# Local attention by halves: row factors in the exponential, rotary rows gathered by transfers, masked copies of two blocks, query weight splits held back

## The chip, the cores and the metric

The kernel runs on one core of a Trainium2 chip. The metric is the device time of one execution in microseconds (us). The engines are named as in the profile: PE is TensorE (PEld its weight load), DVE is VectorE, ACT is ScalarE, POOL is GpSimd, SP is SyncE, which here only issues transfers. Each engine runs its own instructions in the order in which the program issues them; between engines, semaphores order what depends on one another.

## The reference

The reference is the trunk of a small language model with two layers, for 512 tokens with 16 meta tokens ahead of them, 1024 wide. Layer 0 mixes with gated linear attention, layer 1 with local attention over keys and values that are computed once. A gated feed-forward network stands ahead of and behind each mixer, and each part has a norm on its input and one on its output. What the change touches is layer 1's mixer (`hn` is the normalized input; 16 query heads of 64 share 4 key heads; the window is 128 tokens):

```python
q = (hn @ w_q).reshape(B, L, N_KV_HEADS, GROUP, HEAD_DIM)
q = (apply_partial_rope(q, cos, sin) * (HEAD_DIM ** -0.5)).transpose(0, 2, 3, 1, 4)
...
k_band, v_band = band(k), band(v)   # meta keys, previous block, own block
s = jnp.einsum('bkgnqd,bknsd->bkgnqs', q_blk, k_band)
mask = jnp.concatenate([
    jnp.ones((nB, WINDOW, N_META), dtype=bool),
    (j > i)[None] & (blk > 0),
    jnp.broadcast_to((j <= i)[None], (nB, WINDOW, WINDOW)),
], axis=-1)
p = sink_softmax(s, mask, sink)     # exp(s - m) / (sum + exp(sink - m))
o_real = jnp.einsum('bkgnqs,bknsd->bkgnqd', p, v_band)
...
return o @ w_out
```

Of each head's 64 rows the first 16 are turned (`apply_partial_rope`): eight rows with the cosine and sine of the eight others. For query i of a block, the key j of the previous block counts where j > i and that of its own block where j <= i; each column of the two blocks has therefore exactly one of the two visible.

## The kernel before, in words

**Order.** A small planner, `Flow`, holds a clock that each multiplication advances and a heap of jobs, which are generators that yield planned times or other jobs. The main program issues PE's work; whenever the clock passes a job's time, the job issues its next instructions. So constants such as `NORM`, `SOFT` and `LAG` settle where an instruction stands in its engine's queue, and nothing moves once the program is built.

**Weights.** Every float32 weight tile (128 x 512) is loaded by SP into one of 8 raw tiles, and split into a rounded part (ACT, L227) and a remainder (DVE, L228). A product is three multiplications of parts (`mm3s`, L163). Tiles wait in a pool of 32 pairs; `set_ahead(n, slots)` says how far ahead tiles are loaded and how many may be split, and `cap` up to which one.

**Layer 1's mixer, `swa`.** The input `x` is an `Operand`: `build` splits the residual H times the gain into two parts (ACT L429, DVE L430), for two token groups of 256, and `factors` gets each token's row factor 1/rms from sums of squares (`rstd`, small operations on POOL) and broadcasts it by a multiplication (`r_l1m`) to a tile R. `x_first` multiplies the first four units of query weights (128 rows of q each, two heads) group by group, 192 multiplications 256 wide, and `x_units` the last four 512 wide, 96 multiplications. When a unit is done and the row factors are known, `evac` calls `rope`: a shuffle (L1034) and a product (L1035) on DVE, a product and a sum on POOL (L1036, L1037), with tables multiplied by R and 1/8 (L1115).

Then come eight visits, one for each unit u of two heads. `soft(u)` multiplies queries with keys block by block (272 keys, or 144 in the first block), copies the meta keys and the own block (ACT, L1150), and lays the previous block's scores over the own block's where j > i (DVE, a predicated copy, L1151). One row of 144 thus holds all visible keys. Then the maximum (L1156), exponentials with their sums (ACT, L1161), the sink's exponential (L1162), the reciprocal (L1167), and the division, of the meta keys (`mt`, L1169, DVE) and of the rest (L1170, one head on DVE, one on POOL). `core(u)` transposes the probabilities on PE (L175), takes the own and the previous block apart with masks (DVE, L1190 and L1191), copies the meta part (ACT, L1181), multiplies with the values (22 multiplications) and splits the result (ACT L411, DVE L412). Projection work of PE stands between the steps of the visits. `out_proj` multiplies with the output weights, first units 0 to 3 (96 multiplications 512 wide), then 4 to 7 (192 that are 256 wide).

## Time and profile before

| | before |
|---|---|
| median of 3 runs (lowest, highest) | 1932.98 us (1929.79, 1935.67) |
| profiled execution, its own time | 1932.53 us |
| its span | 1930.5 us |
| granted PE clock, mean | 0.992 |
| first multiplication of the query projection | 1390.94 us |
| first 512-wide one of it | 1420.46 us |
| last multiplication of the output projection | about 1561.5 us |

The profile is taken from one execution. Its span goes from the first instruction to the last, and positions in the trace are counted from the span's start. Durations of one instruction contain its start-up, so instructions that follow each other at once overlap a little: a DVE operation of 0.69 us comes every 0.61.

### The profile page before, as it was taken

The numbers are of one execution on the slowest core, as the hardware profiler recorded it, in microseconds if no ns is written. First come the engines' busy times: TensorE is split into PE (matmuls) and PEld (weight loads), VectorE is DVE, ScalarE is ACT, GpSimd is POOL, SyncE is SP. The second block draws the span as 40 slices with busy tenths as digits, with TensorE's granted clock in tenths as the row PEclk, the third lists the DMA queues.
The fourth block names the chain that finished last, engine by engine and source line by source line (L and its number), as shares of the span: only waits on it lengthen the run. The fifth ranks groups of instructions, "written<-read, shape, count | busy, mean of one in ns | idle before, by whom it ended". The sixth has DMA issues, their size and how long they took to land.

```text
span 1930.5 us, 37342 instructions
## 1 busy us (share of the span) xinstructions
PE 1889.1 (98%) x14502; PEld 1801.1 (93%) x14502; DVE 1419.5 (74%) x2868; ACT 1002.5 (52%) x2268; POOL 223.0 (12%) x417
## 2 busy tenths in 40 slices
PE   8999999999999999999999999999998999999997
PEld 8999999999999999999999798989975798989897
DVE  7885858765465798586887786868779678868584
ACT  5553535653245565353574553535646565536363
POOL 2000000321121300000034000000352040000002
PEclk9999999999999999999999999999999999999998
DMA  4223233322113122333351223233321212333331
GB/s 165 91 91 107 91 106 98 123 67 77 56 45 110 56 72 90 106 91 105 99 175 45 66 83 115 91 112 102 123 66 34 69 36 85 95 107 104 105 115 44
DMA packets 102016, 174.61 MB, mean 90 GB/s; under 512 B 11344, under 2 KB 24144, under 8 KB 101840
## 3 DMA queue, kind: packets, MB, share of 16 engines
q1 hardware_dynamic: 101008, 171.59, 28.4%
q8 instruction: 113, 1.85, 0.4%
q10 hardware_dynamic: 832, 0.65, 0.1%
q14 instruction: 63, 0.52, 0.1%
HBM read 170.10 MB, written 2.10 MB: 89 GB/s over the span
## 4 chain that ended last, share of the span: by engine, by line
PE 82%; DVE 12%; ACT 3%; issue 2%; POOL 1%; DMA 0%; SPq 0%; DVEq 0%; ACTq 0%
PE y L163 30%; PE a L163 18%; PE x L163 14%; PE c L163 8%; PE d L163 4%; DVE raw L252 1%; DVE w L228 1%; ACT w_s L246 1%; DVE w_s L247 1%; DVE w L247 1%; PE e L163 1%; PE o L163 1%; PE po L163 1%; DVE xsl0f L723 0%; PE ps L163 0%
## 5 line engine op out<-in xcount | busy, mean ns | idle before, releaser
L247 DVE TENSOR_TENSOR w_s<-raw,w_s 128x512 fp32r<-128x512 f32 x288 | 194.1, 691 | 132.9 <-ACT w_s L246 131.0
L163 PE MATMUL y<-hidl0f,w 128*128 128x272 f32 (+1 forms) x2112 | 264.8, 287 | 3.3 <-ACT hidl0f L411 3.1
L163 PEld LDWEIGHTS y<-hidl0f,w 128*128 128x128 f32 x2112 | 261.7, 190 | 4.4 <-ACT hidl0f L411 3.5
L228 DVE TENSOR_TENSOR w<-raw,w 128x512 fp32r<-128x512 f32 x378 | 243.2, 674 | 17.2 <-ACT w L227 15.4
L163 PE MATMUL y<-hidl1f,w 128*128 128x512 f32 (+1 forms) x1344 | 251.1, 346 | 1.7 <-ACT hidl1f L411 1.4
L246 ACT ACTIVATE w_s<-raw 128x512 fp32r<-128x512 f32 x288 | 175.3, 628 | 145.2 <-DVE raw L252 141.5
L163 PEld LDWEIGHTS y<-hidl1f,w 128*128 128x128 f32 x1344 | 212.3, 188 | 36.6 <-ACT hidl1f L411 2.3
L227 ACT ACTIVATE w<-raw 128x512 fp32r<-128x512 f32 x378 | 208.1, 586 | 35.4 <-PE y L163 27.0
L407 POOL TENSOR_TENSOR acc_post<-acc_post,sq_post 128x256 f32<-128x256 f32 (+1 forms) x72 | 59.1, 821 | 1376.7 <-ACT sq_post L406 1376.1
L252 DVE TENSOR_TENSOR raw<-raw,raw 128x512 f32<-128x512 f32 x288 | 198.3, 688 | 5.5
L247 DVE TENSOR_TENSOR w<-raw,w 128x512 fp32r<-128x512 f32 x216 | 148.6, 688 | 39.5 <-ACT w L246 38.8
L246 ACT ACTIVATE w<-raw 128x512 fp32r<-128x512 f32 x216 | 134.0, 621 | 48.0 <-PE y L163 47.7
L163 PE MATMUL x<-x_l0m,w 128*128 128x272 f32 (+1 forms) x1200 | 158.1, 288 | 0.0
L163 PEld LDWEIGHTS x<-x_l0m,w 128*128 128x128 f32 x1200 | 149.3, 189 | 1.1
L589 DVE TENSOR_TENSOR Y<-y,Y 128x256 f32<-128x256 f32 (+2 forms) x176 | 82.5, 474 | 72.0 <-PE y L163 71.5
L163 PE MATMUL a<-zl0f_t,w_s 128*128 128x264 f32 x864 | 117.3, 285 | 0.0
L163 PE MATMUL a<-zl1f_t,w_s 128*128 128x256 f32 x864 | 114.5, 281 | 0.3 <-ACT c L784 0.2
L163 PEld LDWEIGHTS a<-zl0f_t,w_s 128*128 128x128 f32 x864 | 110.1, 188 | 0.2
L163 PEld LDWEIGHTS a<-zl1f_t,w_s 128*128 128x128 f32 x864 | 107.3, 188 | 1.9 <-ACT c L784 1.5
L163 PE MATMUL x<-x_l0f,w 128*128 128x256 f32 (+1 forms) x768 | 100.4, 291 | 7.2 <-ACT w L227 5.8
L163 PEld LDWEIGHTS x<-x_l0f,w 128*128 128x128 f32 x768 | 97.0, 192 | 8.5 <-ACT w L227 5.8
L163 PE MATMUL x<-x_l1f,w 128*128 128x256 f32 (+1 forms) x576 | 92.7, 320 | 0.0
(483 smaller groups left out, 3308.7 us busy)
## 6 DMA issues: line engine op xcount, KB each, us to landing
raw<-in_w_in SPq DMA_DIRECT2D x352, 256.0 KB, 2.9
raw<-in_w_out SPq DMA_DIRECT2D x96, 256.0 KB, 3.4
raw<-in_gla_in SPq DMA_DIRECT2D x50, 256.0 KB, 2.9
raw<-in_w_last SPq DMA_DIRECT2D x48, 256.0 KB, 3.1
raw<-in_w_out SPq DMA_DIRECT2D x64, 128.0 KB, 2.9
raw<-in_gla_out SPq DMA_DIRECT2D x16, 256.0 KB, 2.7
raw<-in_w_q SPq DMA_DIRECT2D x16, 256.0 KB, 3.9
raw<-in_swa_out SPq DMA_DIRECT2D x16, 256.0 KB, 2.8
```

Of the source, the lines that this page charges most:

```text
L163: inst = pe.matmul(o, lhs, rhs, start=start, stop=stop, skip_group_check=onto)
L227: act.activation(w[:, 0, :m], raw[:, :m], AF.Copy)
L228: dve.tensor_tensor(w[:, 1, :m], raw[:, :m], w[:, 0, :m].bitcast(F32), op=ALU.subtract)
L246: act.activation(w[:, 0, :512], src, AF.Copy)
L247: dve.tensor_tensor(w[:, 1, :512], src, w[:, 0, :512].bitcast(F32), op=ALU.subtract)
L252: dve.tensor_tensor(dst, dst, src, op=ALU.add)
L407: pool.tensor_tensor(sums[0][:, :n], sums[0][:, :n], t[:, :n], op=ALU.add)
L589: dve.tensor_tensor(y, p[:, :n], y, op=ALU.add)
```

## The change

Query rows leave PSUM by an ACT copy with the factor 1/8 (`evac`), without the row factors. `factors` makes only a column of the row factors and of their inverses (`root`), and the row factor is the scale of the exponential; the sink, times the inverse, is a 145th score. The rotary rows, 16 of every 64, are gathered by eight transfers into one packed tile, turned there by four DVE operations, and sent back by eight transfers (`turn`; two groups of 256 for the first four units, one of 512 for the last). The eight visits become sixteen, each a unit by half of the blocks, four units' first halves ahead of their second halves. Scores of two blocks lie in one PSUM tile, so one ACT copy and one predicated copy serve two blocks. The transposed probabilities are copied whole by ACT, and multiplied with the previous block's values; the masked own part goes with the difference of the two blocks' values (`dv`). POOL's part of the division goes to DVE, and so do POOL's two operations of the key's `rope`. The visits are spaced by `PERIOD` and may run `LAG` ahead. The query weights of units 4 to 7 are capped (`cap`) and split within 12 tiles (`held`), and the second half of the output projection waits only for the visits of its tokens (`second`).

The core of the diff; of `swa`, whose old body is shown above, only the new lines:

```diff
-STAGGER = 5.0
-SOFT = 5.0
+SOFT = 6.0
 BEHIND = 2.2
-NORM = 3.0
-LAG = 3
+NORM = 4.0
+LAG = 5
+PERIOD = 5.0
+TURN = 6.0
+PROBS = 2.5
...
-    def rstd(sq, n, dim, half, name, eng=pool, more=0.0):
+    def root(sq, n, dim, name, eng, yv=None, inverse=None):
...
+        if inverse is not None:
+            eng.tensor_tensor(inverse, aa, yy, op=ALU.mult)
+        return yy
+
+    def rstd(sq, n, dim, half, name, eng=pool, more=0.0):
+        yy = root(sq, n, dim, name, eng)
...
         def factors(self, gi, eng=pool):
+            if self.column is not None:
+                o, n = self.groups[gi]
+                yield FACT
+                root(self.accs[gi], n, D, f"{self.name}_{o}", eng, *self.column[gi])
+                yield CHAIN
+                return
...
             for g, p in zip(groups, pst):
-                if all(job.done for job in x.rjob):
+                if raw or all(job.done for job in x.rjob):
                     evac(i, g, p)
...
-    def x_first(x, nu, evac, opening=False, behind=(), first_ahead=8):
+    def x_first(x, nu, evac, opening=False, behind=(), first_ahead=8, held=None):
...
-        set_ahead(8 if opening else 2 * first_ahead)
+        set_ahead(8 if opening else 2 * first_ahead, held)
...
-            yield x.rjob[gi]
+            if x.column is None:
+                yield x.rjob[gi]
...
             if gi == 0 and some[-1] == nu - 1:
-                cap[0] = len(units)
+                if held is None:
+                    cap[0] = len(units)
                 prefetch()
...
         for gi, g in enumerate(split_groups):
+            if gi:
+                flow.wait(*second)
             for m in range(KD - tailm, KD):
...
         dve.stream_shuffle(sh, p, ROT_SHUFFLE)
         dve.tensor_tensor(dst, p, c, op=ALU.mult)
-        pool.tensor_tensor(sh, sh, s, op=ALU.mult)
-        pool.tensor_tensor(dst, dst, sh, op=ALU.add)
+        dve.tensor_tensor(sh, sh, s, op=ALU.mult)
+        dve.tensor_tensor(dst, dst, sh, op=ALU.add)
...
+            dve.tensor_tensor(dv, vt[:, 1:], vt[:, :3], op=ALU.subtract)
...
     def swa(x, kv, finish):
+        kz, vt, dv, vmz = kv
+        cap[0] = used[0] + 8
         with tc.tile_pool(name="ap", bufs=1) as ap:
             mgt = ap.tile([P, P], I32, name="mgt")
             sp.dma_start(mgt, a["mgt"])
+            mle = ap.tile([P, P], F32, name="mle")
             sp.dma_start(mle, a["mle"])
+
             neg = ap.tile([P, P], F32, name="neg")
+            pool.memset(neg, 0.0)
+            for r in (0, 64):
+                pool.memset(neg[r : r + 1], NEG)
             cr, sr = duo("csq")
+            sp.dma_start(cr, a["cosp"])
+            sp.dma_start(sr, a["sinp"])
+            qd = [None] * 4
 
             def evac(u, g, p):
                 o, n = g
+                if qd[u // 2] is None:
+                    qd[u // 2] = pair_tile(f"q{u}", F32)
+                act.activation(qd[u // 2][:, u % 2, o : o + n], p[:, :n], AF.Copy, scale=0.125)
+
+
+            def turn(half, g, after_jobs):
+                for jb in after_jobs:
                     yield jb
+                o, n = g
+                pk, sh = (t[:, o : o + n] for t in duo(f"turn{half}_{o}"))
+                ends = []
+                for d in range(2):
+                    for e in range(2):
+                        for c in range(2):
+                            at = 64 * d + 32 * e + 16 * c
+                            rows = qd[2 * half + d][64 * e : 64 * e + 16, c, o : o + n]
+                            ends.append((rows, pk[at : at + 16]))
+                for rows, packed in ends:
+                    sp.dma_start(packed, rows)
+                yield TURN
+                while (1, KD - 1) not in x.ready:
+                    yield SCORE
+                first = dve.stream_shuffle(sh, pk, TURN_SHUFFLE)
+                after(x.built, first)
+                dve.tensor_tensor(pk, pk, cr[:, o : o + n], op=ALU.mult)
+                dve.tensor_tensor(sh, sh, sr[:, o : o + n], op=ALU.mult)
+                dve.tensor_tensor(pk, pk, sh, op=ALU.add)
+                for rows, packed in ends:
+                    sp.dma_start(rows, packed)
+                yield TURN
+
+
+            visits = [(u, hf) for us in (range(4), range(4, KD)) for hf in range(2) for u in us]
+
+            def score_tile(i):
+                u, hf = visits[i]
+                t = flat(Y)[:, i * 580 : (i + 1) * 580] if i < 7 else flat(pair_tile(f"s{u}_{hf}", F32))[:, :580]
+                return t.rearrange("p (c t) -> p c t", t=145)
+
+            def soft(i, after_jobs):
+                for jb in after_jobs:
+                    yield jb
+                u, hf = visits[i]
                 j = u // 4
+                qq = qd[u // 2][:, u % 2]
+                s = score_tile(i)
+                nm, den = (sm.tile([P, 4], F32, tag=t, name=f"{t}{u}_{hf}", bufs=4) for t in ("nm", "den"))
+
+                rows = [slice(64 * e, 64 * e + 64) for e in range(2)]
+                pa, pb = ([ps(f"s{n}{u}_{hf}{e}") for e in range(2)] for n in "ab")
+                for c in range(2):
+                    b = 2 * hf + c
+                    qs = [qq[rows[e], META + b * P : META + (b + 1) * P] for e in range(2)]
                     for e in range(2):
+                        mm(pa[e][:, c * 144 : (c + 1) * 144], qs[e], kz[j][rows[e], b], cost=0.1)
+                    for e in range(2):
+                        o = pb[e][:, c * P : (c + 1) * P]
+                        if b:
+                            mm(o, qs[e], kz[j][rows[e], b - 1, META:], cost=0.085)
+                        else:
+                            mm(o, ones[rows[e]], neg[rows[e]], cost=0.085)
+                for e in range(2):
+                    t = s[:, 2 * e : 2 * e + 2]
+                    act.activation(t[:, :, :144], pa[e][:, :288].rearrange("p (c k) -> p c k", k=144), AF.Copy)
+                    dve.copy_predicated(
+                        t[:, :, META:144], mgt.unsqueeze(1).to_broadcast([P, 2, P]),
+                        pb[e][:, : 2 * P].rearrange("p (c k) -> p c k", k=P),
+                    )
+                while x.rjob[hf] is None:
                     yield SCORE
+                yield x.rjob[hf]
+
+                rc, ri = x.column[hf]
+                pairs = lambda t: t.rearrange("p (e c) -> p e c", c=2)
+                both = lambda t: t.unsqueeze(1).to_broadcast([P, 2, 2])
+                sinks = vec[:, V_SINK + 2 * u : V_SINK + 2 * u + 2].unsqueeze(2).to_broadcast([P, 2, 2])
+                dve.tensor_tensor(pairs(s[:, :, 144]), sinks, both(ri), op=ALU.mult)
+                dve.tensor_reduce(nm, s, axis=AX.X, op=ALU.max, negate=True)
+                dve.tensor_tensor(pairs(nm), pairs(nm), both(rc), op=ALU.mult)
+                for c in range(4):
+                    act.activation(
+                        s[:, c], s[:, c], AF.Exp, scale=rc[:, c % 2 : c % 2 + 1], bias=nm[:, c : c + 1],
+                        accum_out=den[:, c : c + 1],
+                    )
                 yield SOFT
+                dve.reciprocal(den, den)
+                rd = den.unsqueeze(2)
+                mt = sm.tile([P, 4, META], F32, tag="mt", name=f"mt{u}_{hf}", bufs=4)
+                dve.tensor_tensor(s[:, :, META:144], s[:, :, META:144], rd.to_broadcast([P, 4, P]), op=ALU.mult)
+                dve.tensor_tensor(mt, s[:, :, :META], rd.to_broadcast([P, 4, META]), op=ALU.mult)
+                probs[i] = s, mt
+
+            def core(i):
+                yield softs[i]
                 yield NORM
+                u, hf = visits[i]
                 j = u // 4
+                s, mt = probs[i]
+                pm = ps(f"ptm{u}_{hf}")
+                transpose(pm[:64, :P], mt.rearrange("p c m -> p (c m)"))
+                ptm = sm.tile([64, P], F32, tag="ptm", name=f"pm{u}_{hf}", bufs=2)
+                act.activation(ptm, pm[:64, :P], AF.Copy)
+                p = ps(f"pt{u}_{hf}")
+                for c in range(4):
+                    transpose(p[:, c * P : (c + 1) * P], s[:, c, META:144])
+
+                pt = pair_tile(f"pt{u}_{hf}", F32)
+                pta, ptc = (pt[:, i, :512].rearrange("p (c k) -> p c k", k=P) for i in range(2))
+                pb = p.rearrange("p (c k) -> p c k", k=P)
+                act.activation(pta, pb, AF.Copy)
+                own = (lambda t: t) if hf else (lambda t: t[:, 1::2])
+                dve.tensor_tensor(own(ptc), own(pb), mle.unsqueeze(1).to_broadcast([P, 4 if hf else 2, P]), op=ALU.mult)
+                yield PROBS
+                o = ps(f"o{u}_{hf}")
+
+                kvh = [slice((2 * j + e) * 64, (2 * j + e) * 64 + 64) for e in range(2)]
+                for c in range(2):
+                    b = 2 * hf + c
+                    oo = [o[64 * e : 64 * e + 64, c * P : (c + 1) * P] for e in range(2)]
                     for e in range(2):
+                        mm(oo[e], vt[:, max(b - 1, 0), kvh[e]], pta[:, 2 * e + c], True, False, cost=0.06)
+                    for e in range(2):
                         if b:
+                            mm(oo[e], dv[:, b - 1, kvh[e]], ptc[:, 2 * e + c], False, False, cost=0.06)
+                    for e in range(2):
+                        mm(oo[e], vmz[j][:64, 2 * e + c], ptm, False, True, cost=0.06)
+                if so[u] is None:
+                    so[u] = pair_tile(f"so{u}")
+                split(so[u], o[:, :256], (META + 256 * hf, 256))
 
             so = [None] * KD
+            probs, softs, cores, paces = [None] * 16, [], [], []
+
+
+            def pace(after_jobs):
+                for jb in after_jobs:
+                    yield jb
+                yield PERIOD
+
+            def attend(i, *after_jobs):
+                wait = [*after_jobs, *paces[-1:]]
+                softs.append(flow.spawn(soft(i, wait)))
+                paces.append(flow.spawn(pace(wait)))
+                cores.append(flow.spawn(core(i)))
+
+            drained = x_first(x, 4, evac, held=12)
+            set_ahead(16, 8)
+            turns = [flow.spawn(turn(0, g, [drained[gi]])) for gi, g in enumerate(L1)]
+            for i in range(8):
+                attend(i, turns[i // 4], *cores[max(i - LAG, 0) : max(i - LAG + 1, 0)])
+            x_units(x, 4, L1W, lambda i, g, p: evac(4 + i, g, p))
+            cap[0] = len(units)
+            prefetch()
+            turned = flow.spawn(turn(1, L1W[0], []))
+            for i in range(8, 16):
+                attend(i, turned, cores[i - LAG])
+            flow.wait(*cores[:8])
             out_proj(so[:4], L1W, L1, True, packed=True)
+            flow.wait(*cores[8:12])
             set_ahead(16)
             cap[0] = used[0] + 8
+            out_proj(so[4:], L1W, L1, False, finish, KD, True, second=cores[12:])
 
 
...
         nxt, fin = into("l1m", 1, 1, True, lambda k: gain(1, 2, k), L1)
+        roots = kp.tile([P, 2, 4], F32, name="roots")
+        nxt.column = [(roots[:, 0, 2 * g : 2 * g + 2], roots[:, 1, 2 * g : 2 * g + 2]) for g in range(2)]
         ffn(x, L1W, fin)
...
+TURN_SHUFFLE = [i ^ 8 for i in range(32)]
```

More of the change, by code (lines that the diff above doesn't have):

```diff
@@ L160, in gain, with mm @@
         return vec[:, c : c + 1]
-    def mm(o, lhs, rhs, start=True, stop=True, onto=False):
+    def mm(o, lhs, rhs, start=True, stop=True, onto=False, cost=None):
         inst = pe.matmul(o, lhs, rhs, start=start, stop=stop, skip_group_check=onto)
@@ L166, in mm @@
             n *= d
-        flow.clock += n / 2400 if rhs.dtype == F32R else max(n / 600, 0.12)
+        flow.clock += cost or (n / 2400 if rhs.dtype == F32R else max(n / 600, 0.12))
         return inst
@@ L420, in __init__ @@
             self.rt = rt
+            self.column = None
             self.rjob = [None] * len(groups)
@@ L496, in drain @@
             evac(i, g, p)
+        raw = x.column is not None
         for i in range(nu):
@@ L557, in out_proj, with out_steps @@
             pass
-    def out_steps(hid, groups, split_groups, first, finish=None, tailm=0, packed=False, jobs=()):
+    def out_steps(hid, groups, split_groups, first, finish=None, tailm=0, packed=False, jobs=(), second=()):
         nh = len(hid)
@@ L1194, in core @@
-                yield 0.6
-                o = ps(f"o{u}")
-                for b in range(4):
+                s, mt = probs[i]
[6 more added lines that the diff above has]
+                    transpose(p[:, c * P : (c + 1) * P], s[:, c, META:144])
@@ L1202, in core @@
                         if b:
-                            mm(oo, vt[:, b - 1, kvh], ptp[:, b - 1], False, False)
-                        mm(oo, vmz[j][:, 4 * e + b], ptm, False, True)
-                so[u] = pair_tile(f"so{u}")
-                split(so[u], o, (META, SEQ))
-            so = [None] * KD
-            probs, softs, cores = [None] * KD, [], []
-            def attend(u, *after):
-                softs.append(flow.spawn(soft(u, [*after, *softs[max(u - 2, 0) : max(u - 1, 0)]])))
-                cores.append(flow.spawn(core(u)))
@@ L1215, in swa @@
-            drained = x_first(x, 4, evac, first_ahead=5)
-            for u in range(4):
-                attend(u, *drained)
-            late = x_units(x, 4, L1W, lambda i, g, p: evac(4 + i, g, p))
-            for u in range(4, KD):
-                attend(u, *late, cores[u - LAG])
-            flow.wait(*cores[:4])
+                            mm(oo[e], dv[:, b - 1, kvh[e]], ptc[:, 2 * e + c], False, False, cost=0.06)
+                    for e in range(2):
+                        mm(oo[e], vmz[j][:64, 2 * e + c], ptm, False, True, cost=0.06)
```

112 lines of the change are left out of this document (16 added, 96 removed).

## Prediction

> **What bounds the kernel now.** I read the page's first and fourth parts, then a table of windows over the stage that changes (layer 1's attention, 1380 to 1561 us), then TensorE's timeline there for its gaps, then groups by shape for prices. From the page, busy time by engine and the shares of the chain that ended last:
>
> ```profile
> PE 1889.1 (98%) x14502; PEld 1801.1 (93%) x14502; DVE 1419.5 (74%) x2868; ACT 1002.5 (52%) x2268; POOL 223.0 (12%) x417
> PE 82%; DVE 12%; ACT 3%; issue 2%; POOL 1%; DMA 0%; SPq 0%; DVEq 0%; ACTq 0%
> ```
>
> TensorE (PE) is the bound: 41 us of idle in 1930.5. Any change can only shorten its work, its idle, or its time at a lower clock. The windows (after the bounds and the sum: busy us of PE, weight load, DVE, ACT, POOL; then the granted clock, DMA share, GB/s):
>
> ```profile
> 1420.00:1430.00 10.00, 10.00 (x35) 8.15 (x36) 1.45 (x5) 1.38 (x4) 2.76 (x12) 0.74 0.17 54
> 1430.00:1440.00 10.00, 8.70 (x45) 5.53 (x45) 10.00 (x21) 4.83 (x15) 9.62 (x10) 1.00 0.26 78
> 1450.00:1460.00 10.00, 6.90 (x26) 4.69 (x27) 9.49 (x31) 6.77 (x38) 3.66 (x3) 0.66 0.03 11
> 1460.00:1470.00 10.00, 8.19 (x76) 5.76 (x75) 10.00 (x34) 6.63 (x29) 1.68 (x2) 1.00 0.18 55
> 1480.00:1490.00 10.00, 7.63 (x65) 5.09 (x64) 9.93 (x33) 6.55 (x29) 1.04 (x1) 1.00 0.18 52
> ```
>
> Here DVE is full (9.5 to 10.0 of 10) where PE idles, and twice the clock falls (0.74, 0.66). PE's gaps, from its timeline (start, us, what ran after the gap; in brackets the idle and what ended it):
>
> ```profile
> 1416.28 1.21 PE L163 MATMUL x<-x_l1m,w 128*128 128x256 f32 x8 [1.26 <-ACT x_l1m L429]
> 1418.08 1.02 PE L163 MATMUL x<-x_l1m,w 128*128 128x256 f32 x4 [0.58 <-DVE x_l1m L430]
> 1453.10 0.45 PE L175 MATMUL ptm<-ident,mt 128*128 128x128 f32 x1 [3.54 <-DVE mt L1169]
> 1469.69 0.30 PE L175 MATMUL ptm<-ident,mt 128*128 128x128 f32 x1 [1.81 <-DVE mt L1169]
> 1488.37 0.45 PE L163 MATMUL o<-pt,vt 128*64 128x128 f32 x4 [1.68 <-DVE pt L1190]
> ```
>
> The first two lie in the query projection, where DVE also turns queries; the rest lie in the softmax. Each fall of the clock began just after such gaps (1418.34 and 1452.47) and lasted 6.83 us. Prices, by group (count, then busy us and mean ns of one, then idle before):
>
> ```profile
> L228 DVE TENSOR_TENSOR w<-raw,w 128x512 fp32r<-128x512 f32 x22 | 19.1, 901 | 0.0
> L1151 DVE COPY_PREDICATED s<-mgt,sc 128x128 f32<-128x128 int32 x27 | 6.8, 296 | 1.5 <-ACT s L1150 1.5
> L1037 POOL TENSOR_TENSOR q<-q,sh_q 128x256 f32<-128x256 f32 x8 | 7.0, 871 | 0.6
> L1161 ACT ACTIVATE s<-s,nm 128x144 f32<-128x144 f32 x36 | 14.4, 405 | 4.4 <-DVE nm L1157 4.4
> ```
>
> The weight split takes 0.69 us where POOL is idle, and 901 ns on the mean here: POOL's tensor operations stretch it. The changed kernel takes POOL's rotary and normalizing work out of this stage.
>
> **The sum**, against the profiled execution (1932.53 us: span 1930.5 and 2.0 around it, 0.45 below the median of the runs, 1932.98).
>
> *Ahead of the stage.* The key rotary's two POOL operations go to DVE: two of 0.34 us for each of a few tiles in a stretch where DVE is full, less what POOL's stretching of DVE cost (some 0.4 us for each POOL operation). PE's gap there is 0.41 us. 0, bounds −0.5 and +0.5.
>
> *First projection, 1390.94 to 1420.46.* Queries now leave PSUM by one ACT copy and wait for no row factor, so the second token group's operand builds are no longer queued on DVE behind four shuffles, four products, two products of the tables and POOL's stretching. Gaps: −1.85. The 192 multiplications 256 wide took 23.92 us, at the steady 0.1175 each 22.56: without the low clock −1.36. Statistics and broadcast: the row factors' broadcast (0.24) goes and the rest is no longer at half speed, −0.65. Against it: four query weight tiles are now split in the norm gap before the second group. Three DVE splits of 0.61 (0.69 less overlap) stand in the chain of the last norm; part of it waits for PE anyway: +0.5 (0 to 2). Sum −3.35: the 512-wide projection starts at 1417.1.
>
> *PE's work from there to the last output multiplication* (1420.46 to 1561.5, 141.1 us: 125.4 of work, 10.1 idle, 5.5 lost to the low clock). Scores: 24 pairs 272 wide and 8 of 144, each interrupted by other work, took 21.1; 14 records of 272 in a row took 1.88 us, 0.13 each, and a visit now issues its 16 records (mean 136 columns) in a row, 1.15 each, 18.4: −2.7. Transposes 64+16 instead of 64+8: +0.5. Output of probabilities: the same 176 multiplications in runs half as long: +1.6 (0 to 2). Projections keep their counts. Work 124.1 to 125, I take 124.1 with the projections at 0.231 and 0.242 us: −1.3.
>
> *Idle.* Visits are now 16, a head pair by half the tokens. The first eight run with hardly any projection work between: in program order PE has S0, 24 projection multiplications, S1, 9 more, T0 (transposes), S2, o0, T1, S3, o1, T2 and so on (S scores, o output), then the output projection interleaved with visits 8 to 15. So the chain of a visit is bare. Per visit, in the rows' durations: transposes 0.55, the ACT copy of 512 (0.62), the next visit's four exponentials (405 ns plus 190 for each sum: 1.7 after the first overlap), reciprocal 0.18, normalize 0.69, two predicated copies (296 ns at 128; some 0.42 at two blocks), the meta product 0.22, and handovers of 0.05 to 0.15. That closes at 4.97 us. PE's own work is 3.2 to 3.3 a visit, DVE's 3.5, ACT's 3.2: no engine is full, the dependence sets the period. 1.65 idle for each of visits 4 to 7 and as much around o2 and T4. Before that the first visits are worse: on DVE the mask of visit 1 stands behind six of the eight output weight splits (each 0.61 with its ACT half ahead) and the four operations of the second rotary turn: PE waits 5.85 us at o1 and 2.7 at T2; o0 waits 1.7 for its copy behind the exponentials on ACT. Sum of the gaps 18.4, and 0.8 at the last visit: 19.2, against 10.1: +9.1. Bounds: 12 (the chain at 4.3 and the splits half hidden) and 23.
>
> *Low clock.* Windows of 3.41 us fit the two falls: with 1.86 us of idle in one (the 1.26 and 0.58 gaps), half speed followed for 6.83; with 1.67 or 1.68 in one it did not (the 1.81 gap falls across two). So the gap of 5.85 brings one fall for sure: o1, T2 and S4 at half speed, 1.5 to 2 us; gaps of 1.65 to 1.85 lie at the edge, one more fall at some 1.3: 2.9 in all, against 5.5: −2.6. The Trainium skill ("TensorE: Matmul & The Clock Gate", Part 1) says that the clock drops after a whole idle window of some 3.4 us and advises no idle gap over about 3 us. The trace is stricter: 1.26 and 0.58 us of idle were followed by half speed. By the Trainium skill's rule only the 5.85 gap counts, and the sum would be 1.3 lower.
>
> *Hidden.* The rotary rows go by transfers: eight gathers of 16 rows on SP's queue, four DVE operations, eight transfers back. SP issues one in 0.33 to 0.42 us and they land some 2.9 us later by the medians on the profile's page (of larger transfers), so for the first half 8×0.4+2.9 twice, with 1.4 of DVE: back by 1424.5 and 1428.5, against the first scores at 1431: a margin of 2.5 to 5 us, hidden by the 512-wide projection. Queued behind them on SP are only weight loads not needed before the output projection. The row factor in the exponential's scale costs no instruction; the sink as a 145th column takes the place of three small operations per head. Dropping POOL from the normalizing puts 0.69 per visit on DVE, counted above.
>
> Total: −3.35 −1.3 +9.1 −2.6 = +1.9: 1934.4, say **1934.5**, within 0.3% (5.8 us, about what a measurement of this kernel can tell from no change) of before.
>
> **Rivals.** (1) *Faster: the visits' chain is shorter than 4.97.* I added durations that overlap by an unknown amount. If DVE and ACT hand over as in the 0.05 us rows, and the copy does not push the exponentials, the period is 4.3 and the o1 gap some 4: −4.7 −1.9, and gaps of 1 us bring no second fall, −1.3: 1926.6. For it: DVE and ACT are at 70% of the period. Against: before's mt waits of 1.8 to 3.5 are chains of just this kind.
>
> (2) *Slower: the clock keeps falling.* Each visit has a gap near half a window. If the threshold is met by 1.65 rather than 1.86 of 3.41 us, half speed returns every 2 to 3 visits, and a visit's PE work of 3.25 becomes some 5.5, over its 4.97 period, with longer transposes inside the chain: each fall costs 1.3 to 1.8 and makes the next one likely; four or five falls instead of two, plus gaps widened by 2 or 3 in the first visits: +5 to +8, 1940.5. It decides from gaps of some 1.7 upwards. The Trainium skill's rule excludes it, as no later gap is over 3 us. The trace puts the edge between 49% and 54%.
>
> (3) *Slower: the small transfers are late.* 16 rows each, 1 or 2 KB a row, all on one queue behind five weight loads. With 5 us instead of 2.9 to land, twice, the first scores wait 1 to 2 us beyond the margin; with 7 us some 5, and a fall of the clock follows, 2.5: up to 1942. The trace has no such transfer; its landing times (2.7 to 3.9) speak against.
>
> (4) *The projection's early part gains nothing*, since the extra splits in the norm chain and the ACT copies (eight of 0.4) delay the builds by as much: +2.5, 1937, still within the bound.
>
> **Chances.** Forecast with (4) 0.40, (1) 0.24, (2) 0.23, (3) 0.13. Faster 0.24, same 0.40, slower 0.36. The likeliest case alone spans 1929 to 1938; the range reaches into (1) and (2, 3): 1922 to 1944.
>
> **What would show it.** Right: the 512-wide projection starts near 1417; no gap at its builds; PE's gaps in the first visits end on DVE (mask at visit 1, some 6 us) and on the masks and normalized rows of each later visit, a period near 5 us; POOL nearly empty in the stage; one or two stretches of half clock; no wait of PE for a transfer; output projection without gaps. Wrong: gaps summing to under 12, or more than three falls of the clock, or the first scores waiting for the turn.

## The result: slower, by 0.6%

The changed kernel's median of four executions is 1945.55 us (1939.01 to 1945.96) against 1932.2 for the kernel before on the same chip; the ratio is 1.0062, with a 95% interval of 1.0042 to 1.0082. The execution of 1939.01 us had a mean granted clock of 0.992, the three others 0.988. The profiled one took 1945.37 us with a span of 1943.6, 13.1 us more than before's. From its page, busy time by engine:

```profile
PE 1899.9 (98%) x14634; PEld 1808.5 (93%) x14634; DVE 1398.9 (72%) x2803; ACT 1016.4 (52%) x2262; POOL 182.5 (9%) x379
```

DVE's busy time is 21 us shorter and POOL's 41, as the diff says. But PE is the bound, and its busy time grew by 10.8 us: PE's idle is 43.7 us, hardly more than the 41.4 of before. So the loss is in how long PE's work takes, not mainly in its waits. The windows of the stage and of the stretch behind it (columns as before; PE busy first, the granted clock third from the end):

```profile
1420.00:1430.00 10.00, 10.00 (x45) 8.13 (x44) 1.63 (x5) 0.67 (x2) 2.09 (x11) 1.00 0.16 47
1450.00:1460.00 10.00, 5.98 (x43) 4.04 (x41) 10.00 (x24) 6.18 (x19) 0.00 (x0) 0.67 0.68 213
1460.00:1470.00 10.00, 9.34 (x82) 6.73 (x82) 4.77 (x15) 7.38 (x26) 0.00 (x0) 0.74 0.09 25
1480.00:1490.00 10.00, 8.15 (x78) 6.06 (x78) 7.22 (x20) 6.49 (x23) 0.00 (x0) 0.83 0.01 2
1550.00:1560.00 10.00, 9.02 (x60) 7.27 (x59) 4.01 (x16) 1.95 (x5) 0.00 (x0) 0.69 0.00 0
1590.00:1600.00 10.00, 7.37 (x52) 6.82 (x51) 9.45 (x20) 7.25 (x16) 1.98 (x2) 0.91 0.39 122
```

The fall of the clock at the projection is gone (1420 to 1430: 1.00). In its place the clock falls four times in visits 0 to 7 (0.67, 0.74 and 0.83 twice; 20.5 us at half speed in all), once at visit 15 (6.8 us) and once in the feed-forward network behind (3.4 us). PE's gaps, from its timeline:

```profile
1447.53 0.44 PE L165 MATMUL o<-pt,vt 128*64 128x128 f32 x4 [1.61 <-ACT pt L1250]
1456.27 0.44 PE L165 MATMUL o<-pt,dv 128*64 128x128 f32 x4 [1.09 <-DVE pt L1252]
1460.00 0.42 PE L177 MATMUL ptm<-ident,mt 128*64 128x128 f32 x1 [2.93 <-DVE mt L1230]
1470.90 0.30 PE L177 MATMUL ptm<-ident,mt 128*64 128x128 f32 x1 [1.56 <-DVE mt L1230]
1481.99 0.27 PE L177 MATMUL ptm<-ident,mt 128*64 128x128 f32 x1 [1.64 <-DVE s L1217]
1593.84 1.69 PE L165 MATMUL x<-x_l1f,w 128*128 128x256 f32 x12 [0.86 <-ACT x_l1f L441]
1597.30 4.68 PE L165 MATMUL x<-x_l1f,w 128*128 128x256 f32 x18 [1.77 <-ACT x_l1f L441]
```

The first five are the forecast's gaps at o0, o1, T2, T4 and T6. The last two are in the next stage, of which the forecast says nothing. Where the time went, from the starts and ends of PE's groups in the two profiles (us):

| stretch of PE's work | before | changed | difference |
|---|---|---|---|
| up to the query projection | 1390.94 | 1393.02 | +2.1 |
| its 256-wide part | 29.52 | 26.06 | −3.5 |
| 512-wide part and visits 0 to 7, to the first output projection | 70.45 | 72.32 | +1.9 |
| from there to the last output projection | 70.66 | 79.01 | +8.4 |
| to the last of the next projection (`x_l1f`) | 48.76 | 53.26 | +4.5 |

"Before" has its first output projection where only half of its visits are done too, so the rows compare. The first row is in part an effect of the change. From the first `e<-zl1f` multiplication, in the feed-forward network ahead of the mixer, to the query projection PE takes 221.58 us before, and 222.74 to 222.80 in the twelve profiles of the changed kernel and of those below: 1.2 us more in each. Near 1176 and 1270 two weight loads of the changed kernel wait 0.46 and 0.43 us for the parts of the hidden tile. ACT, which writes the first part (L833), has waited 2.37 us for PE's `y` at 1176, where before it waited for DVE. `dv` holds one of the pool's pairs from the keys on, so the hidden tile may have to wait until `y` has read another; no run tests that. The other 0.9 us vary: at `e<-zl1f` the twelve profiles lie from 1.0 us ahead of before's to 1.5 us behind it.

### The profile page after: what moved, and what is told of

The parts are those of the page before. It is cut to its first block, busy times and chain, and to the rows that moved or that the text cites. A ratio compares the mean times of both kernels' runs of the same rounds, so it can differ in the third digit from the quotient of the medians.

```text
span 1943.6 us, 37592 instructions
## 1 busy us (share of the span) xinstructions
PE 1899.9 (98%) x14634; PEld 1808.5 (93%) x14634; DVE 1398.9 (72%) x2803; ACT 1016.4 (52%) x2262; POOL 182.5 (9%) x379
## 3 DMA queue, kind: packets, MB, share of 16 engines
q8 instruction: 114, 1.87, 0.4%
## 4 chain that ended last, share of the span: by engine, by line
PE 80%; DVE 12%; ACT 4%; issue 2%; POOL 1%; DMA 0%; SPq 0%; DVEq 0%; ACTq 0%
PE y L165 30%; PE a L165 17%; PE x L165 15%; PE c L165 7%; PE d L165 4%; DVE raw L254 2%; ACT w_s L248 2%; DVE w_s L249 1%; DVE w L249 1%; PE o L165 1%; DVE w L230 1%; PE e L165 1%; PE po L165 1%; DVE hidl1f L834 0%; DVE xsl0f L748 0%
## 5 line engine op out<-in xcount | busy, mean ns | idle before, releaser
L230 DVE TENSOR_TENSOR w<-raw,w 128x512 fp32r<-128x512 f32 x378 | 238.3, 660 | 19.9 <-ACT w L229 17.9
L249 DVE TENSOR_TENSOR w<-raw,w 128x512 fp32r<-128x512 f32 x216 | 148.5, 688 | 29.4 <-ACT w L248 28.7
L248 ACT ACTIVATE w<-raw 128x512 fp32r<-128x512 f32 x216 | 134.0, 621 | 41.4 <-PE y L165 41.0
```

The costliest lines, as they stand in the source:

```text
L230: dve.tensor_tensor(w[:, 1, :m], raw[:, :m], w[:, 0, :m].bitcast(F32), op=ALU.subtract)
L248: act.activation(w[:, 0, :512], src, AF.Copy)
L249: dve.tensor_tensor(w[:, 1, :512], src, w[:, 0, :512].bitcast(F32), op=ALU.subtract)
```

## The experiments

**128 rows for the meta part.** In the changed kernel's trace the output multiplications of visits 8 to 11, where nothing waits and the clock is full, are slow: 20 records in 1.69 us, 84 ns each, where before's are 44 in 2.82, 64 ns. Four records take 0.27 next to their like, but 0.36 next to the meta part's. The meta part is multiplied over 64 rows (the profile writes `64*64`), the rest over 128 (`128*64`).

```diff
+            ptms = [ap.tile([P, P], F32, name=f"ptm{r}") for r in range(2)]
+            for t in [*ptms, *(t.rearrange("p c d -> p (c d)") for t in vmz)]:
+                pool.memset(t[64:], 0.0)
...
-                ptm = sm.tile([64, P], F32, tag="ptm", name=f"pm{u}_{hf}", bufs=2)
-                act.activation(ptm, pm[:64, :P], AF.Copy)
+                ptm = ptms[i % 2]
+                act.activation(ptm[:64], pm[:64, :P], AF.Copy)
...
-                        mm(oo[e], vmz[j][:64, 2 * e + c], ptm, False, True, cost=0.06)
+                        mm(oo[e], vmz[j][:, 2 * e + c], ptm, False, True, cost=0.06)
```

> The changed kernel's output multiplications take 90 ns a record on the mean where the clock is full (0.37 us for four of them next to one of the meta tokens, 0.27 between those of the two blocks), before 68 ns. Here the meta part of the output is multiplied over 128 rows, of which 64 are zeros, not over 64. Theory A (each step between multiplications of 128 and of 64 rows costs some 0.1 us, 4 steps a visit): four records take 0.27 everywhere, the 352 records 24 to 25 us at full clock, and the time falls by 3 to 6 us against the changed kernel (1945.5), since part of it lies in PE's gaps. Rival B (the order of the two heads within a block costs it, or the start of each short run): still 90 ns, time within 1 us. Fewer than six falls of the clock are expected by neither.

Measured: 1937.11 us, ratio 1.0024 (1.0014 to 1.0034), 8.4 us less than the changed kernel by the medians and 7.3 by the ratios: more than theory A asked for. One visit's output, first of the changed kernel, then of this one:

```profile
1498.34 0.44 PE L165 MATMUL o<-pt,vt 128*64 128x128 f32 x4
1498.71 0.44 PE L165 MATMUL o<-pm,vmz 64*64 64x128 f32 x4
1499.07 0.44 PE L165 MATMUL o<-pt,vt 128*64 128x128 f32 x4
1499.34 0.39 PE L165 MATMUL o<-pt,dv 128*64 128x128 f32 x4
1499.66 0.43 PE L165 MATMUL o<-pm,vmz 64*64 64x128 f32 x4
1500.03 0.50 PE L165 MATMUL y<-so,w 128*128 128x512 f32 x1
```

```profile
1495.07 0.44 PE L165 MATMUL o<-pt,vt 128*64 128x128 f32 x4
1495.34 0.39 PE L165 MATMUL o<-ptm,vmz 128*64 128x128 f32 x4
1495.56 0.39 PE L165 MATMUL o<-pt,vt 128*64 128x128 f32 x4
1495.78 0.39 PE L165 MATMUL o<-pt,dv 128*64 128x128 f32 x4
1496.00 0.39 PE L165 MATMUL o<-ptm,vmz 128*64 128x128 f32 x4
1496.32 0.97 PE L165 MATMUL y<-so,w 128*128 128x512 f32 x3
```

Read the starts: 1.69 us from the first to the next `y` above, 1.25 below, for the same number of multiplications and twice the rows in the meta part. From the first to the last output projection it takes 73.4 us instead of 79.0; there the 176 records fall from 15.8 to 11.3 us (15.8 holds visit 15 at half speed; at full speed it would be 14.4), and the clock's fall at visit 15 is not there. Four falls are left of the six, which neither theory expected.

The first group takes 0.27 here and the last 0.32, where the others take 0.22. Entering and leaving the output, between `128*128` and `128*64`, costs something too, with 128 rows on both sides: what is priced is a change of the shape that the profile writes, of rows or of columns.

**One step down and up instead of two.** Rows or steps? The meta part stays over 64 rows, but its two runs in a visit are put next to each other. (A kernel with both runs last, for the same question, gave no measurement.)

```diff
+                    def meta(start, stop):
+                        for e in range(2):
+                            mm(oo[e], vmz[j][:64, 2 * e + c], ptm, start, stop, cost=0.06)
+                    if c:
+                        meta(True, False)
                     for e in range(2):
-                        mm(oo[e], vt[:, max(b - 1, 0), kvh[e]], pta[:, 2 * e + c], True, False, cost=0.06)
+                        mm(oo[e], vt[:, max(b - 1, 0), kvh[e]], pta[:, 2 * e + c], not c, bool(c) and not b, cost=0.06)
...
-                    for e in range(2):
-                        mm(oo[e], vmz[j][:64, 2 * e + c], ptm, False, True, cost=0.06)
+                    if not c:
+                        meta(False, True)
```

> As changed, with the meta part still over 64 rows, but last in a half visit's first block and first in its second, so that there is one step from 128 rows to 64 and one back per visit instead of two and two. Theory A (each change between 128 and 64 rows costs some 0.1 us of PE): the 176 records after the first output projection take 75 to 80 ns each where the changed kernel has 90 and the one with 128 rows 64, and the time falls by half of what 128 rows gave, 3 to 5 us, so 1941 to 1943. Rival C (a multiplication over 64 rows is slower by itself): still 88 to 91 ns, time within 1.5 us of 1945.5.

Measured: 1940.72 us, ratio 1.0039 (1.0024 to 1.0054), 4.8 less than the changed kernel by the medians, though the intervals of the ratios overlap. A visit:

```profile
1496.25 0.44 PE L165 MATMUL o<-pt,vt 128*64 128x128 f32 x4
1496.62 0.65 PE L165 MATMUL o<-pm,vmz 64*64 64x128 f32 x8
1497.20 0.44 PE L165 MATMUL o<-pt,vt 128*64 128x128 f32 x4
1497.47 0.39 PE L165 MATMUL o<-pt,dv 128*64 128x128 f32 x4
1497.79 2.35 PE L165 MATMUL y<-so,w 128*128 128x512 f32 x9
```

1.25 us with no step inside, 1.54 with two, 1.69 with four. The fourth leads to the output projection, where the columns change in any case, and adds nothing: 0.15 us for each of the others. The eight records over 64 rows take 0.58 with their step back, so 64 rows are not slow in themselves: theory A, not C. (The mean over all 176 records, 82 ns, is above the 75 to 80 expected since visit 15 still ran at a half clock.) Three such steps in each of 16 visits are 48 times 0.15, some 7 us of PE work at full speed. The Trainium skill states this ("TensorEngine Tiling (Array Packing)", Tiling Modes, Key Properties): changing the tiling mode, unlike changing the tile, drains TensorE. The trace agrees, with 0.15 us a change.

The kernel before had such steps too, between its scores over 64 rows and the projection over 128. From its PE timeline:

```profile
1432.00 1.66 PE L163 MATMUL x<-x_l1m,w 128*128 128x512 f32 x6
1433.60 0.73 PE L163 MATMUL sc<-kz,q 64*128 64x272 f32 x4
1434.25 1.66 PE L163 MATMUL x<-x_l1m,w 128*128 128x512 f32 x6
```

The six 512-wide multiplications take 1.60 us from the first start to the start of the scores. Of 63 in a row in the changed kernel each takes 0.234 (14.76 us), which is 1.41 for six: 0.19 us more beside the scores.

**PE kept busy in the visits.** Extra multiplications, whose result nobody uses, ahead of the transposes of visits 1 to 7 and the output of visits 0 and 1.

```diff
                 pm = ps(f"ptm{u}_{hf}")
+                if 0 < i < 8:
+                    for _ in range(2):
+                        mm(pm[:, 192:512], ident, vt.rearrange("p b v -> p (b v)")[:, :320], cost=1e-6)
...
```

> As changed, with idle PE time filled: two extra multiplications (320 wide, some 0.5 us each, result unused) ahead of the transposes of visits 1 to 7, and two of 256 (0.43 each) ahead of the output of visits 0 and 1. Theory D (falls of the clock after idle of half a window double the price of PE's work in the visits: four falls, 1448 to 1486, some 20 us at half speed): no fall of the clock between 1440 and 1490, the last output of visit 7 some 2 to 5 us earlier relative to the start of the 512-wide projection (72.3 us in the changed kernel). Rival E (the chain of a visit sets its period whatever the clock): the falls vanish but visits 0 to 7 take as long or longer by part of the 8 us of extra work, 72 to 75 us.

Measured: 1944.53 us, ratio 1.0066 (1.005 to 1.0081), as the changed kernel. Two short falls of the clock remain (near 1457 and 1471); in the visits some 7 us run at half speed instead of 20. And yet visits 0 to 7 take 73.4 us, not less than 72.3. Idle and extra work together are 18.0 us (5.0 and 12.9), near the 18.4 us of idle that the forecast put there. That is rival E's reading: at full clock PE would wait for the chain of the next visit instead. By this run alone it is not shown, since the filling may itself have delayed some steps; the next kernel tests it without extra work.

**DVE's weight splits behind the builds.** The 4.5 us of the next stage. There six of DVE's splits (L230) stand ahead of the last two builds (L442) that PE waits for, in the changed kernel's DVE timeline (start, us, line, operation, count; an update of H at 1596.30 left out). The edit limits the split tiles to `slots`, 8 here, in this network's first product:

```profile
1592.94 1.29 DVE L230 TENSOR_TENSOR w<-raw,w 128x512 fp32r<-128x512 f32 x2
1594.14 0.48 DVE L442 SCALAR_TENSOR_TENSOR x_l1f<-H,vec,x_l1f 128x256 fp32r<-128x256 f32 x1
1594.65 1.72 DVE L230 TENSOR_TENSOR w<-raw,w 128x512 fp32r<-128x512 f32 x2
1596.63 1.28 DVE L230 TENSOR_TENSOR w<-raw,w 128x512 fp32r<-128x512 f32 x2
1597.84 0.47 DVE L442 SCALAR_TENSOR_TENSOR x_l1f<-H,vec,x_l1f 128x256 fp32r<-128x256 f32 x1
```

```diff
-        set_ahead(8 if opening else 2 * first_ahead, held)
+        set_ahead(8 if opening else 2 * first_ahead, held or slots)
...
```

> As changed, but in the last feed-forward network only 8 weight tiles may be split until its first product is done, so that four to six of DVE's weight splits come behind the builds of the second token group's operand instead of ahead of them. Theory F (4.4 of the 13 us come from PE's gaps of 0.86 and 1.77 us at those builds and from the half clock that follows): the gaps at the last two builds fall to under 0.6 in sum, no fall of the clock near 1598, 3 to 4.5 us less than the changed kernel (1945.5), so 1941 to 1942.5. Rival G (the builds are late because the output norm of that group is late): gaps of over 2 us remain, time within 1 us.

Measured: 1942.36 us, ratio 1.0057 (1.0037 to 1.0078). The gaps at the builds fall from 2.63 to 0.33 and the next projection ends 49.6 us after the output projection instead of 53.3: theory F, for the builds. But PE then waits 2.36 us for the first hidden tile (0.71 in the changed kernel), and from there to the end of the span it takes 3.3 us longer. By the medians the time is 3.2 us less, but the intervals of the ratios overlap, and no gain from the edit is shown.

This run also tests what half speed costs in the visits. PE's, DVE's and ACT's instructions are the changed kernel's up to 1592 us, but here the first fall of the clock begins at 1456.4 instead of 1448.1. Of visits 0 to 7, 13.7 us run at half speed instead of 20.5; they take 72.7 us instead of 72.3, as idle grows from 9.3 to 13.1. These 6.8 us at half speed cost nothing that the two traces show. In visits 8 to 15, where PE hardly waits (1.0 us in all), the fall lasts 3.4 us instead of 6.8, and they take 77.5 instead of 79.0.

With ten tiles on the 128-row kernel:

> On the kernel with the meta part over 128 rows (1937.1): in the last feed-forward network ten weight tiles may be split until its first product is done (with eight, on the changed kernel, the gaps of 2.6 us at the builds fell to 0.3, but 2.4 came back at the first output product). Theory F (the builds of the second group wait for DVE's weight splits): the gap at the builds (1.78 us with 128 rows) falls below 0.6, no fall of the clock there, 1 to 2.5 us less. Rival G2 (what is held back is missed later): the gap at the first output product grows from 0.7 to over 2 us and the time stays within 1 us.

Measured: 1937.44 us, ratio 1.0026 (1.0016 to 1.0035), no gain over 1937.11: the builds' gap falls from 1.78 to 0.58, the one at the first hidden tile rises from 0.70 to 2.38. Rival G2: the splits can be moved, but someone waits for them later.

**The output projection not split by tokens.** What put the splits there?

```diff
-            flow.wait(*cores[8:12])
+            flow.wait(*cores[8:])
...
-            out_proj(so[4:], L1W, L1, False, finish, KD, True, second=cores[12:])
+            out_proj(so[4:], L1W, L1, False, finish, KD, True)
```

> On the kernel with the meta part over 128 rows (1937.1): the second half of the output projection waits for all visits, not only for those of its tokens, as before the change. Theory L (the loss of 4 us in the feed-forward network behind comes from this split: the first token group's norm runs far ahead of the second's, and the planner then places six weight splits ahead of the second group's last builds): the time from the last output multiplication to the last of the next projection falls from 52.5 to 48.8 to 50 us, with no gap at the builds. Visits 13 to 15, without projection work between them, cost 3 to 5 us more, so the time stays between 1936 and 1939. Rival M (the late builds have another cause): still over 52 us, and 1940 to 1942.

Measured: 1937.04 us, ratio 1.0029 (1.0018 to 1.0041). The next projection takes 48.80 us (before: 48.76), without a gap: theory L. The stretch ahead of it takes 77.4 instead of 73.4, since visits 13 to 15 have no work beside them: among others

```profile
1532.45 0.44 PE L165 MATMUL o<-pt,vt 128*64 128x128 f32 x4 [1.58 <-ACT pt L1253]
1539.53 0.27 PE L177 MATMUL ptm<-ident,mt 128*64 128x128 f32 x1 [1.41 <-DVE mt L1233]
```

So `second` hides 4.0 us and gives 3.7 back in the stage behind.

**The early visits.** Three edits of what stands beside visits 0 to 2, all on the 128-row kernel. First, the output weights loaded and split only from visit 3 on (`cap` raised after `flow.wait(*cores[:3])`):

> On the kernel with the meta part over 128 rows (1937.1): the eight output weight tiles are loaded and split during visits 3 to 7 instead of during visits 0 to 2. Theory H (DVE's queue, full between 1450 and 1460 with weight splits and the second turn, makes the gaps of 3.3 us at the output of visit 1 and 2.6 at the transposes of visit 2): these two fall to under 3 us in sum, and visits 0 to 7 take 2 to 4 us less than 70.4. Rival I (the splits only move: the later visits, or the output projection that waits for its weights, lose as much): sum of the gaps unchanged, time within 1.5 us.

Measured: 1936.68 us, ratio 1.0019 (1.001 to 1.0028): the gap at the output of visit 1 goes, but those at the transposes of visits 2, 4 and 5 are 4.0, 3.2 and 2.8, and visits 0 to 7 take 71.1 us against 70.4. Rival I. Second, `TURN = 5.0`:

> On the kernel with the meta part over 128 rows (1937.1): each planned step of the rotary turn is 1 us shorter, which places the first visit's scores 12 projection multiplications (2.8 us) earlier in PE's order and so puts 21 instead of 9 between the second visit's scores and the first transposes. Theory J (the chain of the first visits is bare since too little projection work stands between them): the gap of 1.6 us at the output of visit 0 vanishes and that at visit 1 shrinks, 1.5 to 3 us less in time. Rival K (the small transfers have not landed by then): the first scores wait for them 0.5 to 2 us and nothing is gained.

Measured: 1933.70 us, ratio 1.0002 (0.9992 to 1.0011): 3.4 us less, visits 0 to 7 in 67.4 us. The gap at visit 0's output is gone, and that at visit 1's is 3.9 instead of 4.8: theory J. (Later expectations put this gap at visit 0; it is visit 1's.) Third, `TURN = 3.0` with the first transfers back on ACT:

> On the kernel with the meta part over 128 rows (1937.1): planned steps of the turn of 3 instead of 6 us, and the first turn's eight transfers back are issued by ACT, idle then, instead of behind the second gather on SP. Scores of the first visit stand 30 projection multiplications (7 us) earlier in PE's order. Theory J (bare chains of the first visits): each projection multiplication that moves between visits 0 to 2 fills gaps (3.6 us at the output of visit 0 and 2.4 at the second transposes were left with 5 us steps): 2 to 4 us less than with 5 us steps (1933.7), 1930 to 1932. Rival K (the transfers land late): PE waits at the first scores for 1 to 3 us, time 1933 to 1936.

Measured: 1935.68 us, ratio 1.0022 (1.0013 to 1.0032). That is 2.0 us more than with steps of 5 us. Scores start another 4.2 us earlier and wait for no transfer, against rival K; but the gap of 3.6 us at visit 1's output stays, one of 1.75 instead of 0.28 follows within the same output, and visits 0 to 7 take 68.4 us. What theory J expected of more projection work did not come; PE's order seems to be no longer what holds them. With the unsplit output projection:

> Both of the other two edits together, on the same kernel. If the gain of the one and the loss of the other are in different places they add: the time of the kernel with 3 us steps plus the difference of the one without the split of the output projection, within 1.5 us. By theory J and L 1929 to 1933.

Measured: 1937.74 us, ratio 1.0033 (1.0024 to 1.0042). The sum of the two would be 1935.6 by the medians, 2.1 us less and so outside the bound given (by the ratios the difference is 1.2 us), and the 1929 to 1933 of theories J and L are missed. The 48.8 us behind and 78.7 ahead are again both there.

**The splits ahead of the visits.** With `TURN = 5.0`, PE waits at visit 1's output for ACT's copy, which starts at 1450.05, behind two weight splits at 1448.85. DVE is nearly idle while PE does the 512-wide projection (1.63 of 10 us, above), so the splits go there.

```diff
-TURN = 6.0
+TURN = 5.0
...
-            set_ahead(16, 8)
+            set_ahead(16, 12)
+            cap[0] = len(units)
+            prefetch()
             turns = ...
...
-            cap[0] = len(units)
-            prefetch()
```

> On the kernel with the meta part over 128 rows and turn steps of 5 us (1933.7): the output weights are released for loading ahead of the visits, with twelve split tiles allowed, so that ten of DVE's and ACT's weight splits lie between 1418 and 1440, where DVE is busy 1.5 to 1.9 of 10 us, and none in visits 1 and 2. Theory H2 (those splits, in ACT's and DVE's queues ahead of the copies and masks of visits 0 to 2, make the gaps of 3.6 at the output of visit 0 and 2.4 at the transposes after it): these fall to under 2 us in sum, and visits 0 to 7 take 63 to 66 us instead of 67.4; 1930 to 1932.5. Rival N (the chain of the visits is what lasts, whatever stands beside it): over 66.5 us, time within 1 us of 1933.7.

Measured: 1931.10 us (12 runs), ratio 0.9994 (0.9985 to 1.0002). From PE's timeline, the first three gaps:

```profile
1446.01 0.44 PE L165 MATMUL o<-pt,vt 128*64 128x128 f32 x4 [0.65 <-ACT pt L1253]
1451.00 0.44 PE L165 MATMUL o<-pt,vt 128*64 128x128 f32 x4 [1.87 <-ACT pt L1253]
1454.18 0.38 PE L177 MATMUL ptm<-ident,mt 128*64 128x128 f32 x1 [1.81 <-DVE mt L1233]
```

At visit 1's output the gap falls from 3.9 to 1.87 and at the transposes of visit 2 from 2.4 to 1.81, while visit 0 waits 0.65. Visits 0 to 7 take 65.1 us. The visits' time and the median are theory H2's and speak against N, though the interval of the ratio overlaps that of `TURN = 5.0` alone; the two gaps named sum to 3.7, not to under 2, so the chain of a visit still keeps some of it. This is the fastest of the kernels run, and level with the one before the change: faster than it could not be shown.

## Why the prediction was wrong, point by point

- **Ahead of the stage and first projection.** At the key's rotary 0 was right: from the first multiplication of the keys' projection to the first `a<-zl1f`, PE takes 98.66 us before and 98.78 in the changed kernel. Behind it 1.2 us were lost in the feed-forward network, which no term held. The projection: −3.35 forecast, −3.46 measured, no gap at its builds, no fall of the clock.
- **PE's work: the step that failed.** The output of probabilities was priced at +1.6 us, bounds 0 and 2, as "runs half as long". It is +4.9 at full speed: 1.69 us for each of eight visits with 20 records and 1.91 for each of eight with 24 are 28.8 us, against 23.9 before. Shorter runs are not what costs it: over 128 rows the same visits take 1.25 and 1.46, 21.7 in all. In place of the forecast's reason the runs showed 0.15 us for each step between 128 and 64 rows, three of them priced in each visit. Before's output had no such step, but its scores had, and the forecast's own comparison there (21.1 us when interrupted, some 1.3 of it lost to half speed, against 18.4 in a row) held part of the price without naming it. Scores (74.5 and 67.3 ns a record 144 and 128 wide in visits 8 to 15, 18.2 us in all) came as forecast, though the row read as 14 records 272 wide holds four that are 144 wide: the timeline joins neighbours of one name. Transposes (9.3) came as forecast.
- **Idle and low clock.** 19.2 and 2.9 us were forecast. Measured from the 512-wide start to the last output projection (151.3 us): idle 10.2; the work at the rates of visits 8 to 14, where the clock was full, 127.2 (x 22.7, y 47.2, output 28.8, scores 18.2, transposes 9.3, statistics 1.0); the rest, 13.9, was lost to half speed (five falls there, 27.3 us). The sum, 24.1, is 2.0 above the forecast (22.1), in other parts: idle 9.0 under it, the clock's loss 11.0 over it. The forecast did not reason that the one would replace the other, so its near sum is in good part luck. So two of the signs that the forecast named for being wrong came: gaps under 12, and more than three falls. PE's longest gap is 2.93 us, so the falls needed no gap over 3. Rival (2), the clock that keeps falling, happened (six falls with the one behind the stage, two before), and after gaps near the size that it named; but in visits 0 to 7 half speed mostly took the place of idle, and was not the price that the rival gave.
- **Places of the gaps.** o0 1.61 (1.7 forecast) and T2 2.93 (2.7) were right; o1 was 1.09 instead of 5.85; PE worked at half speed ahead of it. Where it did not, with the same instructions (`ffn_later`), the two gaps in visit 1's output are 1.06 and 2.95, 4.0 in sum. The period of the later visits is 5.1 to 5.8 us, 4.97 forecast.
- **Transfers.** Hidden, as forecast. But one of 16 rows holds SP for 0.58 us, not 0.33 to 0.42, and lands after 1.9, not 2.9. Rival (3) did not happen.
- **The stage behind.** Not in the sum at all: +4.5 us, caused by `second`, as m_together shows. The diff shows that edit; the forecast followed it only up to the last output projection.
- The forecast, 1934.5, lies 10.9 us below the profiled run: 5 in the stage (3.3 of the output's steps beyond its 1.6, 2.0 of idle and clock), 4.5 behind it, and 2.1 ahead of it (1.2 in the feed-forward network, 0.9 in which executions vary); the rest of the program took back 0.6.

## What to carry to other kernels

When a change alters the shape of small matrix multiplications, count how often the shape changes between neighbours, not only the multiplications: 48 changes cost some 7 us of PE here, where the relief of DVE and POOL in the projection brought 3.5. And look for the price in any row where such a change already happens. When the bound engine has gaps from a chain, work that is slowed inside the gaps can be free, as 6.8 us at half speed were here, and the same outside them is not; price them apart. And follow an edit of the order to the next stage: a wait that is hidden here can return one stage later, where a planner places other work by its new times.

## What was not expected of the hardware

- A step between multiplications over 128 and over 64 rows costs 0.15 us of PE (1.54 against 1.25 us for two, 1.69 for three).
- A single gap of 1.61 us (47% of 3.41) was followed by half speed, while 1.67 us (of the gap of 1.81) and 1.68 us of idle in one window before were not: the length alone does not decide. The fall at visit 15 followed only 0.98 us of idle, in two gaps (0.30 and 0.68). From the visits on, three of the six falls lasted 3.4 us, where both of before's in its stage lasted 6.8.
- A transfer of 16 rows within SBUF holds SP's queue for 0.58 us, longer than one of 256 KB from memory (0.33).
